# Output projection of a two-layer decoder trunk: the last weight block of two token tiles held back, and some weight remainders made on VectorE

## The chip, the cores and the metric

The kernel runs on one core of a Trainium2 chip. The metric is the device time of one execution in microseconds (us).

The engines are named as the profile names them: PE (TensorE, matrix products), PEld (its weight loads), DVE (VectorE), ACT (ScalarE), POOL (GpSimd) and SP (SyncE, which here issues all DMA transfers). Each engine works through its own instructions strictly in order and waits at the first one whose inputs or buffers are not ready.

## The reference

Two layers run over 1024 tokens of 1024 channels. Each layer mixes tokens with four groups of heads (two gated linear recurrences, latent attention, a delta rule), and then channels with a gated MLP. The change touches only the place between the two, here cut to that:

```python
def reference(x, ...):
    for l in range(DEPTH):                       # 2 layers
        h = rms_norm(x, pre_mix_g[l])
        z = h @ w_in[l]
        ...
        mix = jnp.concatenate([o_a, o_b, o_c, o_d], axis=-1) @ w_out[l]   # (1024, 1024) @ (1024, 1024)
        x = x + rms_norm(mix, post_mix_g[l])
        h = rms_norm(x, pre_ffn_g[l])
        y = conv_glu_ffn(h, ffn_w_gate[l], ffn_w_up[l], ffn_conv_w[l], ffn_w_down[l])
        x = x + rms_norm(y, post_ffn_g[l])
    return x
```

Everything is float32. The change concerns `@ w_out[l]`, the two normalisations behind it, and through them the start of the MLP.

## The kernel before, in words

**Precision.** A float32 operand is split into two parts of a type that PE multiplies fast: a high part, made by a cast on ACT (`split`, L197), and a remainder, operand minus high part, made by a subtraction on POOL unless another engine is passed (L198). `mm3` (L209) then makes one product as three matmuls: high times high, high times remainder, remainder times high. A weight block costs one DMA (tile `wst`, two buffers), one cast and one subtraction (both into tiles `wr`), all called from `weight`.

**Tiling of the output projection** (in `mixing`). Tokens are taken in two halves `hf` of four tiles `t` of 128 tokens; the 1024 output columns in two halves `ch` of 512; the 1024 rows of the weight in four blocks `q` of 256 rows, each two steps `k` of 128. One (`hf`, `ch`) is 4 x 4 x 2 x 3 = 96 matmuls into four PSUM banks, one for each token tile; a layer has four of these, 384 matmuls. In three of the four the loop runs over `q` outside and `t` inside, so that each weight block serves all four token tiles. In the last one (`hf` = `ch` = 1) it runs over `t` outside, so that the token tiles end one after the other and their normalisation can start. A weight block is asked for at its first use. Its `wr` tiles take turns in four buffers for each of two pools, so that the cast of a block waits until PE has finished with the block four places earlier.

**Before each half** PE transposes the mixed heads (`split_T`): per token tile two groups of four transposes into a `pm` bank (four such banks), whose high part ACT casts (L317) and whose remainder DVE subtracts (L318), into tiles `f`.

**Behind each token tile**, once its last block is done: ACT copies the PSUM bank (L1188) and sums squares (L230); POOL (first column half) or DVE (second) multiplies by a gain (`half`, L1162); a reciprocal root is made by a small DVE instruction (L238) and a small POOL one (L239); DVE adds the residual (`post_res`, L328), SP stores it. Then comes the norm in front of the MLP (`prenorm_steps`): squares on ACT (L224), reciprocal root (L246 on DVE, L247 on POOL), product on DVE (L286, tile `jh`), eight transposes on PE (L219), copies on DVE or ACT (L301, L305, L307), and for tiles of the first half a cast (ACT) and a subtraction (POOL, `h` L198). The MLP's first products follow on PE; later ones need sums of these tiles (`combine_s2`, tiles `s2h`, `s2l`).

**What sets the order.** The code gives the order of calls only. A scheduler puts every engine's instructions in a fixed order from its own estimates before the program runs, so that a change of the loop or of an engine also moves other instructions.

Of the kernel before, what the change touches and what calls it, by code (L numbers as in the profile page):

```python
# [128 lines left out]
class Body:  # L129
# [67 lines left out]
        self.marks["hi"] = self.nc.scalar.copy(out=hi, in_=src)  # L197
        (eng or self.nc.gpsimd).tensor_tensor(out=lo, in0=src, in1=hi.bitcast(F32), op=ALU.subtract)  # L198

    def weight(self, src, shape, pool="w"):  # L200

        st = self.load(src, shape)
        hi, lo = (self.t(pool, "wr", 4, shape, F32R) for _ in range(2))
        self.split(hi, lo, st)
        return hi, lo

    def mm3(self, out, a, b, start, stop, onto=False):
# [860 lines left out]
    def mixing(self, l, hT, x_src, x_dst):  # L1068
        nc = self.nc
# [89 lines left out]
        def half(y, n, ss):  # L1159
            self.squares(y, n, ss, self.t("f", "fc", 1, None, BF16))  # L1160
            sl = slice(n * 512, (n + 1) * 512)
            (nc.vector if n else nc.gpsimd).tensor_tensor(out=y[:, sl], in0=y[:, sl], in1=gpost[:, sl], op=ALU.mult)  # L1162

        for hf in range(2):
            mT = []
            for t in range(4):
                m = [self.t("m", "f", NFS, [128, 8, 128], F32R) for _ in range(2)]
                self.split_T(lambda k: groups[k // 2][hf][:, t, k % 2 * 128:k % 2 * 128 + 128],
                             lambda q: tuple(p[:, 4 * q:4 * q + 4, :] for p in m))
                mT.append(m)  # L1170
            y = [self.t("z", "z", 8) for _ in range(4)]
            ss = {}
            for ch in range(2):
                cs = slice(ch * 512, (ch + 1) * 512)
                ps = [self.ps([128, 512], "pd") for _ in range(4)]
                ws = [None] * 4

                for t, q in ((t, q) for t in range(4) for q in range(4)) if hf and ch else (
                        (t, q) for q in range(4) for t in range(4)):
                    if (hf, ch, q, t) == (0, 0, 2, 0):  # L1180
                        gpost, gpre = self.gain(l, 1), self.gain(l, 2)
                    if ws[q] is None:
                        ws[q] = self.weight(self.I["wo"][l, ch, q], [128, 2, 512], "m" if q % 2 else "w")
                    for k in range(2):
                        self.mm3(ps[t], tuple(p[:, q * 2 + k, :] for p in mT[t]), tuple(w[:, k, :] for w in ws[q]),
                                 q == 0 and k == 0, q == 3 and k == 1)
                    if q == 3:
                        ev = nc.scalar.copy(out=y[t][:, cs], in_=ps[t])  # L1188
                        if ch == 0:
                            ss[t] = self.t("c", "s2", 8, [128, 2])  # L1190
                            half(y[t], 0, ss[t])
                        else:
                            waiting.append((hf * 4 + t, y[t], ev, ss[t]))

                    if waiting and (t == 3 if hf == 0 or ch == 0 else q == 3) and (hf or q == 3):

                        tt, yt, ev, sq = waiting.pop(0)
                        half(yt, 1, sq)
                        behind[:] = [self.last_sq] if tt > 4 else []
                        self.step(late)  # L1200
                        x = self.post_res(tt, yt, yt, self.rstd2(sq), x_src, x_dst, ev)
                        late.append(self.prenorm_steps(tt, x, gpre, hT2, "f", behind))
                        next(late[-1])
# [496 lines left out]
```

## Time and profile before

| | |
|---|---|
| device time, median of 3 runs | 2949.01 us (2946.44 to 2950.11) |
| the profiled execution, its own device time | 2954.27 us |
| its span, first to last instruction | 2952.5 us |
| PE busy | 2741.6 us, 93% of the span |
| DVE, ACT, POOL busy | 1822.8, 1327.9, 1231.8 us |
| output projection of layer 0, first matmul to first MLP matmul | 713.97 to 822.58 us |
| the same of layer 1 ends at | 2286.92 us |

The span is that of one profiled execution; around it lie 1.8 us. All rows below are of that execution, with times in us from the start of the span.

### The profile page before, as it was taken

To read this page: it belongs to the slowest core of one execution; us is meant where nothing else is said; L and a number is where in the kernel's file an instruction comes from. 1 tells how busy PE (TensorE), PEld (TensorE's weight loads), DVE (VectorE), ACT (ScalarE), POOL (GpSimd) and SP (SyncE) were. 2 spreads that over 40 slices of the span, in tenths; PEclk is the share of its full clock that TensorE was granted. 3 is DMA by queue.
4 is the path that set the end of the run, shared out by engine and by line. 5 is a ranking of instruction groups with operands and counts; after the bars stand their busy time and mean duration, and the time that the engine had idled before them with its cause. 6 is when DMAs were issued, how large, how long until landed. Compare 5 with 4: busy or idle time off the path is not lost. (4 is left out here: it accounts for less than half of the span.)

```text
span 2952.5 us, 39980 instructions
## 1 busy us (share of the span) xinstructions
PE 2741.6 (93%) x14928; PEld 2227.2 (75%) x14928; DVE 1822.8 (62%) x2638; ACT 1327.9 (45%) x2422; POOL 1231.8 (42%) x1030
## 2 busy tenths in 40 slices
PE   7889888899999999999988997988999899999998
PEld 5688676677777888888767875866777688888887
DVE  4764433895487777764556643349935777776645
ACT  4423334655464444454444233355555544444443
POOL 4522453454666454310155225534446755443001
PEclk9999989999999999999999998999999999999999
DMA  5331553112433233376534316421234332223765
GB/s 187 137 108 66 181 190 112 54 60 102 139 122 121 99 102 108 118 264 198 173 137 149 101 56 218 164 101 54 72 103 140 125 118 100 100 99 104 261 194 192
DMA packets 162673, 386.01 MB, mean 131 GB/s; under 512 B 25488, under 2 KB 37040, under 8 KB 162480
## 3 DMA queue, kind: packets, MB, share of 16 engines
q1 hardware_dynamic: 162480, 383.47, 38.9%
q8 instruction: 117, 1.92, 0.3%
q14 instruction: 76, 0.62, 0.1%
HBM read 273.76 MB, written 109.64 MB: 130 GB/s over the span
## 5 line engine op out<-in xcount | busy, mean ns | idle before, releaser
L209 PE MATMUL pd<-h,wr 128*128 128x512 f32 x2608 | 665.0, 405 | 36.4 <-ACT wr L197 27.7
L198 POOL TENSOR_TENSOR wr<-wst,wr 128x512 fp32r<-128x512 f32 (+1 forms) x188 | 353.9, 1886 | 644.8 <-ACT wr L197 635.2
L209 PEld LDWEIGHTS pd<-h,wr 128*128 128x128 f32 x2608 | 492.6, 191 | 155.9 <-ACT wr L197 29.3
L197 ACT CAST wr<-wst 128x512 fp32r<-128x512 f32 (+1 forms) x260 | 196.7, 760 | 314.1 <-PE pd L209 203.9
L209 PE MATMUL pd<-wr,h 128*128 128x256 f32 x1920 | 250.8, 293 | 0.8 <-issue 0.8
L209 PEld LDWEIGHTS pd<-wr,h 128*128 128x128 f32 x1920 | 243.5, 200 | 2.5 <-issue 1.1
L209 PE MATMUL pm<-h,wr 128*128 128x512 f32 x864 | 230.1, 393 | 1.5 <-DVE x L1396 1.5
L198 DVE TENSOR_TENSOR h<-st,h 128x1024 fp32r<-128x1024 f32 x120 | 152.4, 1273 | 120.9 <-ACT h L197 119.8
L209 PE MATMUL pd<-wr,f 128*128 128x512 f32 x768 | 185.4, 398 | 11.6 <-POOL wr L198 10.6
L209 PEld LDWEIGHTS pm<-h,wr 128*128 128x128 f32 x864 | 162.0, 188 | 39.2 <-DVE x L1396 2.5
L197 ACT CAST h<-st 128x1024 fp32r<-128x1024 f32 x120 | 125.7, 1049 | 146.2 <-PE pd L209 83.0
L209 PE MATMUL pd<-h 128*128 128x512 f32 x816 | 185.6, 389 | 0.0
L209 PEld LDWEIGHTS pd<-wr,f 128*128 128x128 f32 x768 | 143.7, 189 | 45.0 <-POOL wr L198 12.4
L209 PEld LDWEIGHTS pd<-h 128*128 128x128 f32 x816 | 153.2, 188 | 31.8
L1334 DVE SCALAR_TENSOR_TENSOR g<-z,pp,g 128x512 f32<-128x512 f32 x176 | 164.3, 933 | 20.8 <-ACT g L1332 18.0
L209 PE MATMUL pm<-h 128*128 128x512 f32 x720 | 166.2, 391 | 0.5 <-DVE h L198 0.5
L1455 POOL TENSOR_TENSOR y<-y,gb 128x512 f32<-128x512 f32 x24 | 38.2, 1598 | 304.2 <-ACT fc L230 179.3
L209 PEld LDWEIGHTS pm<-h 128*128 128x128 f32 x720 | 135.6, 189 | 29.1 <-DVE h L198 1.0
L215 PE MATMUL pm<-g,g 128*128 128x128 f32 (+1 forms) x672 | 121.4, 329 | 30.9 <-issue 12.9
L215 PEld LDWEIGHTS pm<-g,g 128*128 128x128 f32 x672 | 99.4, 201 | 59.1 <-issue 28.9
L1552 POOL TENSOR_TENSOR d<-d,d 128x512 f32<-128x512 f32 x64 | 109.4, 1709 | 54.4 <-DMA d<-in_wgu_dram 49.0
L209 PE MATMUL pd<-hs,wr 128*128 128x512 f32 x528 | 128.4, 393 | 1.4 <-ACT x L1400 1.4
(364 smaller groups left out, 5428.0 us busy)
## 6 DMA issues: line engine op xcount, KB each, us to landing
st<-gd SPq DMA_DIRECT2D x144, 256.0 KB, 3.2
gd<-g SPq DMA_DIRECT2D x88, 256.0 KB, 2.0
d<-in_wdn_dram SPq DMA_DIRECT2D x40, 512.0 KB, 5.4
td<-d SPq DMA_DIRECT2D x40, 512.0 KB, 2.6
st<-td SPq DMA_DIRECT2D x80, 256.0 KB, 3.6
ust<-in_wgu_dram SPq DMA_DIRECT2D x36, 512.0 KB, 3.8
wst<-in_wgu_dram SPq DMA_DIRECT2D x36, 512.0 KB, 3.6
st<-in_wdn_dram SPq DMA_DIRECT2D x68, 256.0 KB, 3.5
```

Of the source, the lines that this page charges most:

```text
L197: self.marks["hi"] = self.nc.scalar.copy(out=hi, in_=src)
L198: (eng or self.nc.gpsimd).tensor_tensor(out=lo, in0=src, in1=hi.bitcast(F32), op=ALU.subtract)
L209: mm = lambda x, y, **k: self.nc.tensor.matmul(out, lhsT=x, rhs=y, skip_group_check=onto, **k)
L215: self.nc.tensor.matmul(out, lhsT=lhsT, rhs=rhs, start=start, stop=stop)
L1334: nc.vector.scalar_tensor_tensor(out=c, in0=x[:, j:j + 512], scalar=w(j), in1=c, op0=ALU.mult, op1=ALU.add)
L1455: (dve if last and n else pool).tensor_tensor(out=y[t][:, c], in0=y[t][:, c], in1=g_post[:, c], op=ALU.mult)
L1552: sub = lambda o, x, y: nc.gpsimd.tensor_tensor(out=o, in0=x, in1=y, op=ALU.subtract)
```

## The change

The loop of the last quarter (`hf` = `ch` = 1) takes blocks 0 to 2 for token tile 0, then for token tile 1, then block 3 for both; token tiles 2 and 3 go as before. `weight` gets an argument for the engine that makes the remainder: POOL for blocks 0 to 2 in the second half of the tokens, DVE for the eight blocks of the first half and for block 3 of both column halves in the second. So 10 of a layer's 16 weight remainders move from POOL to DVE.

```diff
-    def weight(self, src, shape, pool="w"):
+    def weight(self, src, shape, pool="w", eng=None):
 
         st = self.load(src, shape)
         hi, lo = (self.t(pool, "wr", 4, shape, F32R) for _ in range(2))
-        self.split(hi, lo, st)
+        self.split(hi, lo, st, eng)
         return hi, lo
...
-                for t, q in ((t, q) for t in range(4) for q in range(4)) if hf and ch else (
+
+                for t, q in [(t, q) for t in (0, 1) for q in range(3)] + [(0, 3), (1, 3)] + [
+                        (t, q) for t in (2, 3) for q in range(4)] if hf and ch else (
                         (t, q) for q in range(4) for t in range(4)):
...
-                        ws[q] = self.weight(self.I["wo"][l, ch, q], [128, 2, 512], "m" if q % 2 else "w")
+                        ws[q] = self.weight(self.I["wo"][l, ch, q], [128, 2, 512], "m" if q % 2 else "w",
+                                            nc.gpsimd if hf and q < 3 else nc.vector)
```

PE, the end of the first column of work in the last quarter, layer 0, before (`pd_6859` and `pd_6860` are the banks of token tiles 0 and 1; `wr_6889`/`wr_6890` are high part and remainder of block 2, `wr_6901`/`wr_6902` of block 3, `wr_6865` is block 0; `f_6560`/`f_6561` are tile 0's own parts; `jh_6791` is a token tile of the first half):

```order
L209 MATMUL pd_6859<-wr_6889,f_6561 128x512
L209 MATMUL pd_6859<-wr_6901,f_6560 128x512
L209 MATMUL pd_6859<-wr_6902,f_6560 128x512
L209 MATMUL pd_6859<-wr_6901,f_6561 128x512
L209 MATMUL pd_6859<-wr_6901,f_6560 128x512
L209 MATMUL pd_6859<-wr_6902,f_6560 128x512
L209 MATMUL pd_6859<-wr_6901,f_6561 128x512
L219 MATMUL pm_6915<-cf,jh_6791 128x128 x4
L219 MATMUL pm_6923<-cf,jh_6791 128x128 x4
L209 MATMUL pd_6860<-wr_6865,f_6576 128x512
```

The same place of the changed kernel, where block 3 is `wr_6919`/`wr_6920` and 18 matmuls of token tile 1 stand ahead of it (the last of them is the first row):

```order
L209 MATMUL pd_6860<-wr_6889,f_6577 128x512
L209 MATMUL pd_6859<-wr_6919,f_6560 128x512
L209 MATMUL pd_6859<-wr_6920,f_6560 128x512
L209 MATMUL pd_6859<-wr_6919,f_6561 128x512
L209 MATMUL pd_6859<-wr_6919,f_6560 128x512
L209 MATMUL pd_6859<-wr_6920,f_6560 128x512
L209 MATMUL pd_6859<-wr_6919,f_6561 128x512
L219 MATMUL pm_6933<-cf,jh_6791 128x128 x4
L219 MATMUL pm_6941<-cf,jh_6791 128x128 x4
L209 MATMUL pd_6860<-wr_6919,f_6576 128x512
```

The block 3 products of token tile 0 now stand 36 instead of 18 matmuls behind the start of the quarter, and those of tile 1 six matmuls and eight transposes behind them.

POOL at the same place, before (`z_6624` to `z_6627` are the four token tiles of the second half, first 512 columns):

```order
L198 TENSOR_TENSOR h_6201<-h_6197,h_6200 128x4x128
L1162 TENSOR_TENSOR z_6624<-z_6624,gb_6334 128x512
L1162 TENSOR_TENSOR z_6625<-z_6625,gb_6334 128x512
L1162 TENSOR_TENSOR z_6626<-z_6626,gb_6334 128x512
L198 TENSOR_TENSOR wr_6902<-wst_6899,wr_6901 128x1024
L1162 TENSOR_TENSOR z_6627<-z_6627,gb_6334 128x512
L198 TENSOR_TENSOR h_6199<-h_6194,h_6198 128x4x128
```

And of the changed kernel:

```order
L198 TENSOR_TENSOR h_6201<-h_6197,h_6200 128x4x128
L1162 TENSOR_TENSOR z_6624<-z_6624,gb_6334 128x512
L1162 TENSOR_TENSOR z_6625<-z_6625,gb_6334 128x512
L1162 TENSOR_TENSOR z_6626<-z_6626,gb_6334 128x512
L1162 TENSOR_TENSOR z_6627<-z_6627,gb_6334 128x512
L198 TENSOR_TENSOR h_6199<-h_6194,h_6198 128x4x128
```

The remainder of block 3 (`wr_6902`) has left POOL's queue; on DVE its successor `wr_6920` stands behind three one-column instructions (L232) of the same quarter.

DVE at the border between the two halves, where the eight transposed groups of the second half are taken out of their `pm` banks (L318, `f_6561` to `f_6609`), the difference (- before, + changed):

```order
-L318 TENSOR_TENSOR f_6561<-pm_6562,f_6560 128x512
 L318 TENSOR_TENSOR f_6561<-pm_6569,f_6560 128x512
-L328 SCALAR_TENSOR_TENSOR z_6267<-z_6267,rs_6672,x_6675 128x1024
 L318 TENSOR_TENSOR f_6577<-pm_6578,f_6576 128x512
 L318 TENSOR_TENSOR f_6577<-pm_6585,f_6576 128x512
 L318 TENSOR_TENSOR f_6593<-pm_6594,f_6592 128x512
 L318 TENSOR_TENSOR f_6593<-pm_6601,f_6592 128x512
+L328 SCALAR_TENSOR_TENSOR z_6267<-z_6267,rs_6672,x_6675 128x1024
```

The first group (`pm_6562`) is now transposed near the start of the first half and taken out before the border, and the residual addition L328 stands behind five of the other groups instead of ahead of them.

## Rows read from the trace of the kernel before

**Rows 1.** The page: span, busy times, one group of instructions (mean ns).

```profile
span 2952.5 us, 39980 instructions
PE 2741.6 (93%) x14928; PEld 2227.2 (75%) x14928; DVE 1822.8 (62%) x2638; ACT 1327.9 (45%) x2422; POOL 1231.8 (42%) x1030
...
L198 DVE TENSOR_TENSOR h<-st,h 128x1024 fp32r<-128x1024 f32 x120 | 152.4, 1273 | 120.9 <-ACT h L197 119.8
```

**Rows 2.** Windows, layer 0's last quarter: PE, PEld, DVE, ACT, POOL busy; PEclk; DMA.

```profile
796.00:799.60 3.60, 0.00 (x0) 0.00 (x0) 0.00 (x0) 0.00 (x0) 3.60 (x4) 1.00 0.00 0
799.60:803.60 4.00, 3.98 (x15) 3.40 (x16) 0.96 (x2) 1.70 (x4) 1.20 (x1) 0.59 0.40 131
803.60:822.50 18.90, 18.90 (x95) 15.68 (x94) 14.11 (x17) 9.75 (x20) 12.52 (x11) 1.00 0.33 112
```

**Rows 3.** Timeline of PE, output projection: start, us, instruction [idle before <-what ended it].

```profile
716.38 43.79 PE L209 MATMUL pd<-wr,f 128*128 128x512 f32 x189 [1.48 <-POOL wr L198]
...
762.41 0.74 PE L209 MATMUL pd<-wr,f 128*128 128x512 f32 x2 [0.50 <-ACT f L317]
764.69 0.66 PE L219 MATMUL pm<-cf,z 128*128 128x128 f32 x4 [1.54 <-DVE f L318]
...
768.48 0.66 PE L219 MATMUL pm<-cf,z 128*128 128x128 f32 x4 [1.06 <-DVE f L318]
...
799.62 1.97 PE L209 MATMUL pd<-wr,f 128*128 128x512 f32 x5 [3.84 <-POOL wr L198]
801.39 1.91 PE L219 MATMUL pm<-cf,jh 128*128 128x128 f32 x8
802.95 6.14 PE L209 MATMUL pd<-wr,f 128*128 128x512 f32 x24
808.93 1.03 PE L219 MATMUL pm<-cf,jh 128*128 128x128 f32 x8
809.72 5.78 PE L209 MATMUL pd<-wr,f 128*128 128x512 f32 x24
...
2263.99 2.00 PE L209 MATMUL pd<-wr,f 128*128 128x512 f32 x5 [3.82 <-POOL wr L198]
```

**Rows 4.** Timelines of ACT and POOL around block 3 of the last quarter.

```profile
792.35 1.05 ACT L197 CAST wr<-wst 128x1024 fp32r<-128x1024 f32 x1
...
793.51 3.75 POOL L1162 TENSOR_TENSOR z<-z,gb 128x512 f32<-128x512 f32 x3
797.22 2.34 POOL L198 TENSOR_TENSOR wr<-wst,wr 128x1024 fp32r<-128x1024 f32 x1
```

**Rows 5.** Timeline of DVE: the residual addition twice, at the border of the halves.

```profile
759.42 1.28 DVE L328 SCALAR_TENSOR_TENSOR z<-z,rs,x 128x1024 f32<-128x1024 f32 x1 [0.67 <-POOL rs L239]
...
765.14 2.68 DVE L328 SCALAR_TENSOR_TENSOR z<-z,rs,x 128x1024 f32<-128x1024 f32 x1
```

**Rows 6.** Timelines of ACT, POOL and DVE behind token tile 0, last quarter.

```profile
801.63 0.59 ACT L1188 COPY z<-pd 128x512 f32<-128x512 f32 x1 [7.61 <-PE pd L209]
...
803.90 3.00 POOL L198 TENSOR_TENSOR h<-h,h 128x512 fp32r<-128x512 f32 x2 [3.10 <-ACT h L197]
...
809.13 0.59 ACT L1188 COPY z<-pd 128x512 f32<-128x512 f32 x1 [4.45 <-PE pd L209]
...
812.42 1.28 DVE L286 SCALAR_TENSOR_TENSOR jh<-z,rs,gb 128x1024 f32<-128x1024 f32 x1 [0.60 <-POOL rs L247]
```

**Rows 7.** Timelines of POOL and PE, start of the MLP, layer 0 and layer 1.

```profile
850.30 0.58 POOL L1331 COPY tails<-z 128x2 f32<-128x2 f32 x1 [4.19 <-DVE z L1396]
851.90 0.80 PE L209 MATMUL pd<-s2h,wr 128*128 128x512 f32 x1 [4.24 <-ACT s2h L197]
879.09 2.96 PE L209 MATMUL pm<-h,wr 128*128 128x512 f32 x12
...
2314.66 10.81 POOL L1331 COPY tails<-z 128x2 f32<-128x2 f32 x1 [4.19 <-DVE z L1396]
2350.08 2.94 PE L209 MATMUL pm<-h,wr 128*128 128x512 f32 x12
```

## The prediction

> **What bounds the kernel now.** I read the page first: PE is busy for 2741.6 of 2952.5 us [rows 1], so only a stretch in which PE stands still, or runs at its lower clock, can give time back, and the other engines matter where PE waits for them. The change touches nothing but the output projection of each layer, so next I read PE's timeline there. In layer 0 the reader is to see five waits [rows 3]: 1.48 us at the start for the first weight remainder from POOL; 0.50, 1.54 and 1.06 us at the border between the token halves, for casts and subtractions that free transpose banks; and 3.84 us in the last quarter, again for a remainder from POOL. Layer 1 has the last one too, with 3.82 us [rows 3]. In 796.0 to 799.6 us PE, DVE and ACT all do nothing and POOL alone is busy [rows 2].
>
> Then POOL and ACT ahead of that wait [rows 4]. The high part of block 3 is cast from 792.35 to 793.40 us; then POOL spends 793.51 to 797.26 us on three gain products that nobody waits for yet, and only then makes the remainder, which ends at 799.56 us. PE goes on at 799.62 us. So the wait is a matter of POOL's order, not of the DMA or the cast.
>
> The clock row follows: 1.00 in the wait, 0.59 on average in the 4 us behind it, 1.00 after that [rows 2]. PE fell to its 1.2 GHz level behind the wait and came back to 2.4 GHz about three us later.
>
> Last I read what lies behind the projection: PE waits 4.24 us for `s2h` at 851.90 us [rows 7], the end of a chain through ACT, DVE and POOL that starts at the last token tile. A gain in the projection is worth only as much as this chain moves with it.
>
> **The change part by part, for one layer.**
>
> *The wait in the last quarter.* In the changed order block 3 is needed after 36 matmuls instead of 18. A matmul in an unbroken run takes 43.79 / 189 = 0.232 us [rows 3], so it would be needed 4.2 us after PE now stops (799.62 - 3.84 = 795.78), at 799.9 us. Ready it is earlier: the cast still ends at 793.4, and the subtraction takes 1.27 us on DVE, by 120 instructions of that size [rows 1], against 2.34 us on POOL [rows 4]; DVE is idle there [rows 2]. That is 794.7 us, five us to spare. The wait of 3.84 us goes; a bound on the other side is that DVE is held up by more than five us, for which no row speaks. What stands behind the new DVE instruction is one one-column instruction and then the copies of the next transposes, which come seven us later: costs nothing.
>
> *The clock behind it.* The next 5 matmuls took 1.97 us against 5 x 0.232 and some 0.25 for the last one's drain, 1.41: 0.56. The 8 transposes took 1.91 against 1.03, the 24 matmuls 6.14 against 5.78, by the next ones of their kind [rows 3]. Sum 0.56 + 0.88 + 0.36 = 1.8 us, which goes with the wait (bounds 0 and 1.8).
>
> *The start.* The first remainder moves from POOL (2.34 us [rows 4]) to DVE (1.27 us [rows 1]): 1.1 us of the 1.48 us wait. One matmul and four transposes, moved up ahead of it, fill what is left. I take 1.1 (bounds 0, if DVE's two late subtractions behind it now hold PE, and 1.48).
>
> *The border of the halves.* PE waits 0.50 + 1.54 + 1.06 = 3.1 us [rows 3]. The first wait goes, since the first transposed group is now taken out beforehand, so that six matmuls of token tile 0 can run at once. The second stays: PE reaches it sooner, but its bank is freed behind the same norm chain on DVE; I put 1.9 us. The third goes: the bank it waited for was freed behind the residual addition that took 2.68 us [rows 5] and is now freed ahead of it. Four transposes fewer stand there, at 1.03 us for 8 about 0.4 us. So 3.1 - 1.9 + 0.4 = 1.6 us (bounds 0 and 3.1).
>
> *The seven other remainders of the first half* meet an almost idle DVE and no PE wait: the 189 matmuls run without a break [rows 3]; POOL gains 7 x 2.34 us that no one waits for. Nothing. On SP one residual load moves ahead of one weight load and one behind, in a stretch without a wait for a DMA: nothing.
>
> *What is late next.* So far PE gains 3.84 + 1.8 + 1.1 + 1.6 = 8.3 us. But token tile 0 now ends 18 matmuls later, and PE asks for its normalised rows (transposes of `jh`) 8 transposes, 6 matmuls, 8 transposes and 24 matmuls behind: 0.8 + 1.4 + 0.8 + 5.6 = 8.6 us after its end. Today the chain from the copy at 801.63 us to the end of the product L286 at 812.42 + 1.28 takes 12.1 us, hidden because a whole tile more lies between [rows 6]. It will be shorter: ACT held the chain back until 809.13 us, where the next tile's copy stood in front of the squares [rows 6], and that tile now ends 2.2 us after tile 0. Two subtractions on POOL of 3.00 us together still stand in front of the reciprocal root [rows 6], and now two tiles share DVE. Adding up the steps I get 10.6 to 11.2 us, so a new wait of 2.0 to 2.6 us; I take 2.3. Bounds: 0, and 12.1 - 8.6 = 3.5 us. Whether the clock falls behind it is open: 1.54 us did not bring it down, 3.84 us did [rows 2, 3]; that would be up to 1.8 us more. I leave it out of the sum and in the range.
>
> *Handing on.* 8.3 - 2.3 = 6.0 us for a layer. The rest of the chain to `s2h` hangs on the token tiles' ends and on loads that are issued behind them, nothing on a fixed time, so I let 6.0 us pass on whole.
>
> **Sum.** Two layers, 12.0 us: the profiled execution would go from 2954.3 to 2942.3 us. The median of the runs shown is 5.3 us under that execution, so the forecast is 2949.0 - 12.0 = **2937.0 us**.
>
> **A lock that could undo part of it.** At the start of the MLP POOL copies two columns (`tails`). In layer 0 that took 0.58 us, in layer 1, at the same distance from the wait in the projection (50.68 and 50.67 us), 10.81 us [rows 3, 7], while DVE ran without a gap. What it cost: from the wait in the projection to the twelve matmuls that follow later is 879.09 - 799.62 = 79.47 us in layer 0 and 2350.08 - 2263.99 = 86.09 us in layer 1, 6.6 us more. Likewise the residual addition took 1.28 us alone and 2.68 us where POOL was at work [rows 5]. The Trainium skill (SBUF — State Buffer, Who interferes with whom) says that a DVE instruction with two SBUF inputs and a GpSimd instruction that reads SBUF shut each other out for the whole instruction, whoever starts first. The trace agrees in kind. By that rule every remainder moved to DVE becomes one that can shut POOL out, which speaks against the change; by the rows of the first half, where POOL has little left to do, it costs nothing.
>
> **The rivals.**
> (A) The forecast, 12 us less, its own range 2933 to 2941 us: 50%.
> (B) The norm chain of tile 0 is short enough and no new wait comes: 2 x 8.3 = 16.6 us, 2932.4 us. For it speaks that three of the chain's steps were waiting in line today; against it, that two tiles now come at once. 12%.
> (C) As A, but a `tails` copy falls the other way than in a typical run. One more is shut out: 2937.0 + 6.6 = 2943.6 us, 14%. One fewer: 2930.4 us, 8%. The order there is unchanged, only the moment shifts, and layers 0 and 1 show that the moment decides.
> (D) The gain ends at the wait for `s2h`: DVE's chain there does not come sooner, and PE waits 4.24 + 6.0 us instead. No change, 2949 us. For it: PE waits there today. Against it: DVE had 18.90 - 14.11 us of idle time in the last quarter [rows 2], so it follows the tiles. 10%.
> (E) Slower: with two tiles at once DVE works without a gap while POOL's small reciprocal root (L239) needs its turn, and is shut out as the copy was, for 10.81 - 0.58 = 10.2 us [rows 7]. It decides from 6.0 us in each layer on; at 10.2 us the sum is 2 x (10.2 - 6.0) = 8.4 us, 2957.4 us. Against it: DVE has had gaps in this stretch every few us. 6%.
>
> **How the numbers follow.** Predicted is A. A difference of 0.2%, 5.9 us, is about what a measurement of this kernel can tell from no change. Faster by more (below 2943.1 us) are A, B, the good side of C and almost half of its bad side: 0.74. Within 0.2% are D and the rest of C: 0.20. Slower is E: 0.06. For the range I leave out D above 2946 and E, and the tail under 2927 us: 2927 to 2946 us holds A, B and both sides of C.
>
> **What the profile will show.** Right: no PE wait of over 1 us for a POOL `wr` in the projection, and a granted clock of 1.00 there in the last quarter; the three waits at the border down to one of about 1.9 us; a wait of about 2.3 us for `jh` L286 ahead of the transposes behind token tile 2; the first MLP matmul of layer 0 some 6 us earlier than 822.58 us, the one on `s2h` some 6 us earlier than 851.90 us. Wrong: a wait for block 3 that merely names DVE instead of POOL; a `jh` wait of over 3.5 us, or a clock of 0.5 behind it; `s2h` at 851.9 us as before; a `tails` copy of 10 us in both layers.

## The result and the profile after

The changed kernel takes 2934.59 us (median of 4 runs, 2932.39 to 2936.43) where the kernel before took 2949.56 us beside it (4 runs, 2946.44 to 2955.0). The ratio is 0.9943, with a 95% interval of 0.9927 to 0.9958: faster by 15 us. The forecast was 2937.0 us.

The page after, against [rows 1]; the profiled execution took 2936.43 us:

```profile
span 2934.6 us, 39974 instructions
PE 2736.2 (93%) x14928; PEld 2224.1 (76%) x14928; DVE 1838.8 (63%) x2658; ACT 1328.4 (45%) x2422; POOL 1187.8 (40%) x1010
```

With the 20 remainders that moved, POOL has lost 44 us of work and DVE has gained 16 us. PE lost only 5.4 us of busy time; the rest of the 18 us by which the span is shorter was waiting.

PE's timeline of the output projection after, layer 0 and then layer 1, against [rows 3, 7] (start, us, instruction, and in brackets the idle time before it and what ended it):

```profile
713.52 1.43 PE L209 MATMUL pd<-wr,f 128*128 128x512 f32 x4
...
715.15 43.53 PE L209 MATMUL pd<-wr,f 128*128 128x512 f32 x188
...
763.16 0.66 PE L219 MATMUL pm<-cf,z 128*128 128x128 f32 x4 [1.32 <-DVE f L318]
...
774.20 1.03 PE L219 MATMUL pm<-cf,jh 128*128 128x128 f32 x8
...
781.44 15.44 PE L209 MATMUL pd<-wr,f 128*128 128x512 f32 x66
796.71 1.03 PE L219 MATMUL pm<-cf,jh 128*128 128x128 f32 x8
...
799.76 5.81 PE L209 MATMUL pd<-wr,f 128*128 128x512 f32 x24
808.03 1.06 PE L219 MATMUL pm<-cf,jh 128*128 128x128 f32 x8 [2.46 <-DVE jh L286]
...
815.27 5.72 PE L209 MATMUL pd<-h,wr 128*128 128x512 f32 x24
...
844.76 0.79 PE L209 MATMUL pd<-s2h,wr 128*128 128x512 f32 x1 [4.23 <-ACT s2h L197]
...
858.18 1.22 PE L209 MATMUL pd<-s2h,wr 128*128 128x512 f32 x2 [6.84 <-POOL wr L198]
...
2170.94 1.43 PE L209 MATMUL pd<-wr,f 128*128 128x512 f32 x4
...
2265.41 1.06 PE L219 MATMUL pm<-cf,jh 128*128 128x128 f32 x8 [2.46 <-DVE jh L286]
...
2272.63 5.73 PE L209 MATMUL pd<-h,wr 128*128 128x512 f32 x24
```

The wait at the start is gone, the border has one wait instead of three, and 66 matmuls run without a break through the place where block 3 was waited for. In return there is one new wait, of 2.46 us for `jh`, ahead of the transposes behind token tile 2. The clock did not fall behind it (columns as in [rows 2], PEclk third from the end):

```profile
781.40:796.70 15.30, 15.30 (x69) 12.46 (x68) 5.60 (x10) 8.25 (x18) 14.02 (x9) 1.00 0.46 156
796.70:808.00 11.30, 8.87 (x47) 7.15 (x45) 7.89 (x12) 7.05 (x15) 6.57 (x7) 1.00 0.24 74
808.00:815.30 7.30, 7.27 (x41) 6.22 (x41) 6.68 (x7) 4.51 (x9) 4.70 (x5) 1.00 0.50 175
```

From here on a **stretch** is the time from the first matmul of a layer's projection to the first MLP matmul (the first `pd<-h,wr` row), both starts read from PE's timeline. Before it is 822.58 - 713.97 = 108.6 us, and 108.6 us in layer 1; after it is 815.27 - 713.52 = 101.7 us, and 2272.63 - 2170.94 = 101.7 us. It holds all four quarters and the new wait. In the traces of kernels with the same order of the projection it repeats to 0.1 us (table below), where the whole time spreads over 4 to 18 us in the runs of one kernel; so it is the better measure of this change.

The chain of token tile 0's normalisation, ahead of the new wait; timelines of ACT, DVE and POOL after, in order of time, against [rows 4, 6]:

```profile
788.21 1.05 ACT L197 CAST wr<-wst 128x1024 fp32r<-128x1024 f32 x1
789.29 1.23 DVE L198 TENSOR_TENSOR wr<-wst,wr 128x1024 fp32r<-128x1024 f32 x1 [0.86 <-ACT wr L197]
...
796.91 0.59 ACT L1191 COPY z<-pd 128x512 f32<-128x512 f32 x1 [7.03 <-PE pd L209]
798.84 2.81 POOL L198 TENSOR_TENSOR h<-h,h 128x512 fp32r<-128x512 f32 x2 [3.42 <-ACT h L197]
801.60 0.55 POOL L239 TENSOR_TENSOR rs<-rs,nhalf 128x1 f32<-128x1 f32 x1
802.19 2.31 DVE L328 SCALAR_TENSOR_TENSOR z<-z,rs,x 128x1024 f32<-128x1024 f32 x1 [1.89 <-POOL rs L239]
804.53 1.06 ACT L224 ACTIVATE jh<-z 128x1024 f32<-128x1024 f32 x1 [3.49 <-DVE z L328]
806.02 0.55 POOL L247 TENSOR_TENSOR rs<-rs,nhalf 128x1 f32<-128x1 f32 x1 [2.59 <-DVE rs L238]
806.60 1.28 DVE L286 SCALAR_TENSOR_TENSOR jh<-z,rs,gb 128x1024 f32<-128x1024 f32 x1 [0.61 <-POOL rs L247]
```

From the copy to the end of L286 it takes 806.60 + 1.28 - 796.91 = 11.0 us. The two subtractions on POOL that nobody hurries for (798.84) stand in front of the reciprocal root L239 again.

### The profile page after: what moved, and what is told of

Its sections match the earlier page's. It is cut to its first block, busy times and chain, and to the rows that moved or that the text cites. A ratio compares the mean times of both kernels' runs of the same rounds, so it can differ in the third digit from the quotient of the medians.

```text
span 2934.6 us, 39974 instructions
## 1 busy us (share of the span) xinstructions
PE 2736.2 (93%) x14928; PEld 2224.1 (76%) x14928; DVE 1838.8 (63%) x2658; ACT 1328.4 (45%) x2422; POOL 1187.8 (40%) x1010
## 5 line engine op out<-in xcount | busy, mean ns | idle before, releaser
L198 POOL TENSOR_TENSOR wr<-wst,wr 128x512 fp32r<-128x512 f32 (+1 forms) x168 | 307.9, 1837 | 616.1 <-ACT wr L197 606.7
L1337 DVE SCALAR_TENSOR_TENSOR g<-z,pp,g 128x512 f32<-128x512 f32 x176 | 164.2, 933 | 20.4 <-ACT g L1335 17.9
L198 DVE TENSOR_TENSOR wr<-wst,wr 128x512 fp32r<-128x512 f32 (+1 forms) x92 | 95.9, 1043 | 101.5 <-ACT wr L197 101.5
```

Of the source, the lines that this page charges most:

```text
L1337: nc.vector.scalar_tensor_tensor(out=c, in0=x[:, j:j + 512], scalar=w(j), in1=c, op0=ALU.mult, op1=ALU.add)
```

## The experiments

"Before" is the median of the kernel before, run in the same set; the stretches are those of the profiled execution.

| kernel | median us | before | ratio (95%) | stretch, layer 0 / 1 |
|---|---|---|---|---|
| changed | 2934.59 | 2949.56 | 0.9943 (0.9927 to 0.9958) | 101.7 / 101.7 |
| e1 engine moves only | 2930.78 | 2954.23 | 0.9929 (0.9910 to 0.9949) | 99.1 / 99.1 |
| e2 order only | 2947.89 | 2954.23 | 0.9983 (0.9970 to 0.9997) | 105.6 / 105.5 |
| e3 block 3 on DVE only | 2945.45 | 2954.23 | 0.9971 (0.9956 to 0.9986) | 105.8 / 103.0 |
| e4 first half on DVE only | 2944.66 | 2954.23 | 0.9969 (0.9957 to 0.9981) | 104.8 / 105.0 |
| e5 changed, again | 2939.70 | 2953.82 | 0.9952 (0.9937 to 0.9967) | 101.7 / 101.7 |
| e6 as e1, again | 2933.84 | 2953.82 | 0.9932 (0.9918 to 0.9946) | 99.1 / 99.1 |
| e7 changed, `tails` on ACT | 2936.57 | 2953.82 | 0.9937 (0.9923 to 0.9951) | 101.7 / 101.7 |
| e8 as e1, `tails` on ACT | 2929.76 | 2953.82 | 0.9923 (0.9909 to 0.9936) | 99.1 / 99.1 |
| e9 as e1, other additions | 2935.87 | 2952.78 | 0.9947 (0.9930 to 0.9965) | 99.1 / 99.1 |
| e10 as e8, other additions | 2931.11 | 2952.78 | 0.9931 (0.9915 to 0.9947) | 99.1 / 99.1 |
| e11 as e1, third time | 2933.26 | 2952.78 | 0.9939 (0.9921 to 0.9956) | 99.1 / 99.1 |

### Which part clears the wait: the order or the engine?

The prediction priced the later place of block 3 and its move to DVE as one term. Its own numbers held a rival: the remainder on DVE would end at 794.7 us, and PE came to it at 795.8 us even in the old order. Four kernels take the two apart.

**e1**, the changed kernel with the old loop:

```diff
-                for t, q in [(t, q) for t in (0, 1) for q in range(3)] + [(0, 3), (1, 3)] + [
-                        (t, q) for t in (2, 3) for q in range(4)] if hf and ch else (
+                for t, q in ((t, q) for t in range(4) for q in range(4)) if hf and ch else (
```

> Edit: the ten remainders stay on DVE, but the loop of the last quarter is the old one, token tile by token tile, so nothing is held back. Theory 1 (holding back is what clears the wait for block 3): block 3 is needed after 18 matmuls again and the wait comes back, over 1 us for `wr` from DVE instead of POOL, with the clock behind it; 2940 to 2945 us, slower than the changed kernel by 5 to 10 us. Theory 2 (the engine alone clears it, since the subtraction on DVE ends about 794.7 us and PE comes to it at 795.8 us in the trace before): no wait over 0.3 us for block 3, no clock drop, and the wait for `jh` of 2.46 us behind token tile 2 goes too; 2 x 2.5 = 5 us under the changed kernel, about 2930 us. PE now reaches block 3 some 3.3 us earlier against the trace before, by the shorter start and border, which is the weak place of Theory 2: if DVE's end does not move with it, a wait of up to 2 us is left there.

Timelines of PE and DVE in e1, layer 0:

```profile
712.61 1.43 PE L209 MATMUL pd<-wr,f 128*128 128x512 f32 x4
...
780.51 11.28 PE L209 MATMUL pd<-wr,f 128*128 128x512 f32 x48
788.34 1.23 DVE L198 TENSOR_TENSOR wr<-wst,wr 128x1024 fp32r<-128x1024 f32 x1 [0.87 <-ACT wr L197]
...
804.46 1.04 PE L219 MATMUL pm<-cf,jh 128*128 128x128 f32 x8
...
811.70 5.73 PE L209 MATMUL pd<-h,wr 128*128 128x512 f32 x24
```

Theory 2 holds. Token tile 0 runs through all its 24 matmuls inside an unbroken run of 48, although the remainder of block 3 ends only at 789.57 us. Of these 48 matmuls 24 belong to the quarter before, 18 to blocks 0 to 2, and the first of block 3 takes only the high part; so the remainder is asked for at 780.51 + 43 x 11.28 / 48 = 790.6 us, 1.0 us behind its end. And the transposes at 804.46 us wait for no `jh`. The stretch is 99.1 us in both layers, 2.6 us shorter than with the block held back. The time, 2930.78 us, is what Theory 2 asked for, though the kernel before took 4.7 us more in this set than in the first.

**e2**, the opposite: the new loop, all remainders on POOL.

```diff
-                                            nc.gpsimd if hf and q < 3 else nc.vector)
+                                            nc.gpsimd)
```

> Edit: the new loop order, but all 16 remainders of a layer on POOL as before. Theory 1 (holding back clears the wait): the remainder ends at 799.6 us as before and is needed at 799.9 us, so the wait is under 0.5 us and the clock holds, worth 5.6 us in a layer; the start (1.48 us) and the border (3.1 us) wait as before, and `jh` waits some 2.5 us more: 3.1 us a layer, about 6 us under the kernel before, 2943 us. Theory 2 (the engine is what counts): a wait for block 3 of over 1 us stays in place, and no gain is left after the `jh` wait, 2948 to 2952 us.

PE's timeline in e2, layer 0:

```profile
713.61 43.86 PE L209 MATMUL pd<-wr,f 128*128 128x512 f32 x189 [1.47 <-POOL wr L198]
...
782.93 15.50 PE L209 MATMUL pd<-wr,f 128*128 128x512 f32 x66
...
809.59 1.06 PE L219 MATMUL pm<-cf,jh 128*128 128x128 f32 x8 [2.46 <-DVE jh L286]
```

As Theory 1 had it: the order clears the wait for block 3 too (66 matmuls without a break), though only just: POOL makes the remainder from 794.56 us in 2.40 us, and it is asked for at 782.93 + 61 x 15.50 / 66 = 797.3 us. The start waits as before, and `jh` costs 2.46 us. The stretch is 3.0 us shorter than before, the time 6.3 us. So the order alone clears the wait, and so do the ten moves alone; the order is paid for with `jh`, the moves with nothing that the stretch shows.

**e3** moves nothing but block 3 of the second half, in the old loop; PE's order is that of before.

```diff
-                                            nc.gpsimd if hf and q < 3 else nc.vector)
+                                            nc.vector if hf and q == 3 else nc.gpsimd)
```

> Edit: the old loop order, and only block 3 of the two quarters of the second half of the tokens has its remainder made on DVE; PE's order is that of the kernel before, instruction by instruction. Theory 2 (the engine alone clears the wait): 3.84 us and the 1.8 us at the low clock behind it go in both layers, nothing else changes, no `jh` wait: 2 x 5.6 = 11.3 us under the kernel before, about 2938 us. Theory 1 (it has to be held back as well): the wait stays, over 1 us, 2944 us or more.

PE's timeline in e3, layer 0 (with DVE's remainder of block 3), then layer 1:

```profile
766.40 2.91 PE L209 MATMUL pd<-wr,f 128*128 128x512 f32 x6
...
792.79 4.41 PE L209 MATMUL pd<-wr,f 128*128 128x512 f32 x18 [0.73 <-ACT z L1190]
797.42 0.50 PE L209 MATMUL pd<-wr,f 128*128 128x512 f32 x1 [0.22 <-ACT wr L197]
797.41 1.23 DVE L198 TENSOR_TENSOR wr<-wst,wr 128x1024 fp32r<-128x1024 f32 x1 [0.89 <-ACT wr L197]
798.69 1.43 PE L209 MATMUL pd<-wr,f 128*128 128x512 f32 x5 [0.76 <-DVE s L232]
...
2256.62 1.42 PE L209 MATMUL pd<-wr,f 128*128 128x512 f32 x5 [0.76 <-DVE s L232]
```

The result lies between the theories, in time too (8.8 us under the kernel before, where Theory 2 asked for 11.3): 3.84 us became 0.76 us in both layers, and the clock stayed up behind it (1.42 us for the 5 matmuls instead of 1.97). The releaser named is a one-column instruction on DVE (L232); what PE needs there is the remainder just ahead of it in DVE's queue, which ends at 797.41 + 1.23 = 798.64 us. In layer 1 the stretch is 5.6 us shorter than before, but not by block 3 alone: the third wait at the border, 1.07 us in layer 1 before, is gone from that trace too. Layer 0 is some 2.8 us longer than layer 1: six matmuls at the border took 2.91 us, at a granted clock of 0.75 to 0.83 in 764 to 772 us, and ACT, which had waited until 782.38 us for the load of a weight block, came late with the bank (0.73 us) and the cast (0.22 us). So the move of block 3 alone is late by 0.76 us. With the other eight moves (e1) PE's and ACT's order changes as well, and nothing is left; which of these changes closes the gap no run shows.

**e4** moves only the eight remainders of the first half, in the old loop.

```diff
-                                            nc.gpsimd if hf and q < 3 else nc.vector)
+                                            nc.gpsimd if hf else nc.vector)
```

> Edit: the old loop order, and only the eight remainders of the first half of the tokens on DVE; block 3 stays on POOL. The start and the border are all that change. By the account of the trace after, they gave some 3.5 us a layer on PE, but the wait for block 3 stands behind them: if POOL's end of that remainder (799.56 us) follows PE, 2 x 3.5 = 7 us under the kernel before, about 2942 us; if POOL's order there is set by work that does not start earlier, the wait of 3.84 us grows by what the border gave, and nothing is left, 2948 to 2950 us.

Timelines of POOL and PE in e4, layer 0:

```profile
785.16 3.74 POOL L1162 TENSOR_TENSOR z<-z,gb 128x512 f32<-128x512 f32 x3
788.86 2.34 POOL L198 TENSOR_TENSOR wr<-wst,wr 128x1024 fp32r<-128x1024 f32 x1
791.26 1.53 PE L209 MATMUL pd<-wr,f 128*128 128x512 f32 x5 [3.89 <-POOL wr L198]
```

The first alternative: the wait stays at 3.89 us, as long as before, because POOL's queue starts earlier with PE. Start and border alone give 3.8 and 3.6 us of the stretch, and 9.6 us of the time where 7 were expected. e4 and e1 differ in the code only in the engine of block 3, so this move is worth 104.8 - 99.1 = 5.7 us, and 5.9 us in layer 1, wait and clock together.

### Is the hold-back a loss in the whole time, and what is a `tails` copy worth?

The next four ran in one set. `tails` is the copy on POOL that the prediction's rival C was about.

```diff
-                    nc.gpsimd.tensor_copy(out=ends[f], in_=x[:, 512:514])
+                    nc.scalar.copy(out=ends[f], in_=x[:, 512:514])
```

> Edit: none, the changed kernel as it is, timed beside the three others of this set. Expected: 0.9943 of the kernel before again, with the interval of 0.9927 to 0.9958 seen first. Which of the two layers has its `tails` copy shut out by DVE may differ; the two layers' projections, 131.2 us from the first matmul to the first one on `s2h`, may not, by more than 0.3 us.

> Edit: as the first experiment (ten remainders on DVE, old loop order), to be timed beside the changed kernel. Theory 2 (holding back is not needed, and only brings the wait for `jh`): in the traces the stretch to `s2h` is 128.4 and 128.8 us against 131.2 us, so 2 x 2.6 = 5.2 us under the changed kernel, 0.9925 of the kernel before. Theory 1 (in time the two are alike, since what comes earlier is waited for at `tails` or later): within 2 us of the changed kernel, 0.994.

> Edit: the changed kernel with the copy of two columns (`tails`) on ACT instead of POOL. Theory A (a DVE without a gap shuts POOL's copy out, and PE then waits 7 us for the `wr` behind it): no such wait in either layer; 10 us shorter from the first matmul on `s2h` to the first on `hs` in a layer that was shut out, of which the trace of after against before says 3.5 us last to the end; with half the copies shut out in a usual run, 3.5 to 7 us under the changed kernel, 2928 to 2931 us. Theory B (whatever POOL starts next is shut out in its place): a `wr` subtraction on POOL takes 10 us there instead, PE waits as before, and the time stays within 2 us of the changed kernel.

> Edit: the old loop order with the ten remainders on DVE, and `tails` on ACT. If the two gains add up (2 x 2.6 us by the order, 3.5 to 7 us by the copy): 9 to 12 us under the changed kernel, about 2923 us, 0.990 of the kernel before, and the best of all. If the copy is worth nothing, as the first of these two alone, 2929 us.

The stretches repeat to 0.1 us. Up to the first matmul on `s2h`, e5 took 131.2 us in layer 0 as expected, but 131.8 us in layer 1, over the 0.3 us allowed: one more wait for `jh`, of 0.53 us, stands in the MLP's first products there. Side by side the kernel without the hold-back is 5.9 us faster (2933.84 against 2939.70 us), 6.8 us with `tails` on ACT (2929.76 against 2936.57 us), where the stretches say 2 x 2.6 = 5.2 us. The intervals of each pair still overlap, and the means of the six runs differ by 5.8 and 4.6 us with standard errors of 2.3 and 1.7 us; what carries the conclusion is that both pairs and both layers' stretches agree.

With `tails` moved the medians are 3.1 us (e7 against e5) and 4.1 us (e8 against e6) lower, about the low end of what Theory A asked for. By the means it is 4.3 and 3.1 us, with standard errors of 2.2 and 1.8 us, so neither pair by itself is clear of the noise. The timelines of e7 say why it is not more (POOL and PE, layer 0):

```profile
848.50 12.61 POOL L198 TENSOR_TENSOR wr<-wst,wr 128x512 fp32r<-128x512 f32 x3 [6.85 <-ACT wr L197]
857.79 1.22 PE L209 MATMUL pd<-s2h,wr 128*128 128x512 f32 x2 [3.79 <-POOL wr L198]
```

The copy is off POOL, and now the `wr` subtractions are the ones that are shut out: the first of the three took 9.24 us by itself, all three 12.6 us, and PE waits 3.79 us, where it waited 6.84 us after. Theory B was right that the next instruction on POOL is shut out in the copy's place, but not that PE waits as long as before; Theory A was right about part of the gain, if the 3 to 4 us hold. e8 has the lowest ratio of the study, 9.9 us under the changed kernel as expected (9 to 12 us), though its ratio is 0.9923 and not 0.990, and its interval overlaps those of e1, e6 and e11.

### What lets POOL through?

In the traces of before, after, e1 and e11 the copy that was shut out ended within 0.15 us of the moment when DVE came to its first SCALAR_TENSOR_TENSOR (L1337 of the changed kernel) behind a row of TENSOR_TENSORs; timelines of POOL and DVE after, layer 0:

```profile
843.16 10.82 POOL L1334 COPY tails<-z 128x2 f32<-128x2 f32 x1 [4.18 <-DVE z L1399]
...
846.63 1.88 DVE L1272 TENSOR_TENSOR h<-h,h 128x512 f32<-128x512 f32 x3
...
853.86 0.73 DVE L1337 SCALAR_TENSOR_TENSOR g<-z,pp,g 128x512 f32<-128x512 f32 x1
```

So e9 and e10 make four of these TENSOR_TENSORs instructions of the other kind, e9 in e1's kernel and e10 in e8's:

```diff
-                dve.tensor_tensor(out=s1[:, k, :], in0=s1[:, k, :], in1=a22[:, k, :], op=ALU.add)
+                dve.scalar_tensor_tensor(out=s1[:, k, :], in0=s1[:, k, :], scalar=1.0, in1=a22[:, k, :], op0=ALU.mult, op1=ALU.add)
```

> Edit: old loop order with the ten remainders on DVE, and the four additions of DVE in the MLP's start (`s1` plus `a22`) written as multiply by 1.0 and add, which is another kind of DVE instruction with the same result; every engine's order stays as it was. Theory A (a row of DVE instructions of the one kind, TENSOR_TENSOR, shuts POOL out as long as it lasts; POOL gets through at the first instruction of another kind): `tails` on POOL takes about 3.6 us instead of 10.8 us, up to the first of these additions, PE's wait for the POOL `wr` behind it falls from 7.0 us to under 3 us, and some 4 to 7 us a layer come back there, of which 2 to 4 us last: 4 to 8 us under the same kernel without this edit. Theory B (it is the two SBUF inputs that shut POOL out, of either kind of instruction): `tails` takes 10.8 us as before, and the time stays within 2 us.

> Edit: as the one ahead of it, and `tails` on ACT. Theory A: the three `wr` subtractions on POOL that follow take 5 to 8 us instead of 12.6 us, PE's wait for them falls from 4.6 us to under 2 us; 2 to 4 us a layer, 4 to 8 us under the kernel with `tails` on ACT alone, the best of all at about 2922 to 2926 us. Theory B: 12.6 us as before, no change against 0.9923.

> Edit: the first experiment once more, as the base of the two others of this set: 0.993 of the kernel before, `tails` shut out in one or both layers.

Timelines of POOL in e9, layer 0, and then of DVE and POOL in e10, layer 0:

```profile
836.45 5.39 POOL L1333 COPY tails<-z 128x2 f32<-128x2 f32 x1 [4.19 <-DVE z L1398]
...
843.94 1.88 DVE L1271 SCALAR_TENSOR_TENSOR h<-h,h 128x512 f32<-128x512 f32 x3
843.14 12.60 POOL L198 TENSOR_TENSOR wr<-wst,wr 128x512 fp32r<-128x512 f32 x3 [6.85 <-ACT wr L197]
851.16 1.75 DVE L1336 SCALAR_TENSOR_TENSOR g<-z,pp,g 128x512 f32<-128x512 f32 x1
852.84 6.83 DVE L198 TENSOR_TENSOR s<-h,h 128x512 fp32r<-128x512 f32 x4
855.70 6.83 POOL L198 TENSOR_TENSOR wr<-ust,wr 128x512 fp32r<-128x512 f32 x4
```

Theory A falls: in e10 POOL's first subtraction (843.14 us, 9.23 us by itself) sat through all four of the rewritten additions, the three at 843.94 us and one later, up to L1336 at 851.16 us. The three subtractions took 12.60 us, as in e8 (12.62), and PE waited 4.26 us for them where the theory asked for under 2. In e9 the copy took 5.39 us in layer 0, let through right behind the additions, but 10.81 us again in layer 1, past the same four. The kind alone does not decide. Why POOL comes through at that instruction each time (L1337, in e10 L1336; its scalar is a column of a tile and not a constant, and it follows work of ACT) stays open. Nor did any run take the row of DVE instructions away: that DVE is what holds POOL is read from the times alone. In time e9 and e10 gained nothing: 2935.87 against 2933.26 us for e11, and a ratio of 0.9931 against 0.9923 for e8.

## Why the prediction was right, and where its terms were off

**The wait in the last quarter and the clock behind it.** Forecast 3.84 + 1.8 = 5.6 us; measured alone (e1 against e4) 5.7 and 5.9 us. Right in size. The forecast "five us to spare" was right too: the remainder ended at 789.29 + 1.23 = 790.5 us and was needed at about 795.7 us, behind 61 of the 66 matmuls. What was not asked is whether all five were needed. They were not: 1.0 us to spare, without the hold-back (e1), did as well.

**Start and border.** Forecast 1.1 + 1.6 = 2.7 us; measured alone (e4) 3.8 and 3.6 us. This is the term that was mis-sized. The start gave what was forecast: from the first matmul to the end of the first half's 192nd it took 716.38 + 43.79 - 713.97 = 46.2 us before and 715.15 + 43.53 - 713.52 = 45.2 us after, the four transposes included. The border gave more: from there to the first transposes of `jh` it took 18.2 us before (they began at 778.40 us) and 15.5 us after, 2.7 us instead of 1.6. Of that, 0.6 us is the wait that stayed, 1.32 us where 1.9 was put down; the remaining half microsecond I can't put to one row.

**The new wait for `jh`.** Forecast 2.3 us within 0 and 3.5; measured 2.46 us in both layers, in the forecast place, with the clock at 1.00 behind it. It costs 2.6 us of the stretch (changed against e1). That the clock would stay up was left open, and one reason given for it is weaker than it looked: the prediction read that 1.54 us of waiting did not bring the clock down. In the traces of before, e2 and e3 the same wait at the border, 1.53 or 1.54 us, stands six times; five times the granted clock stayed at 1.00, and in e3, layer 0, it fell to 0.72 in the two us from 765.11 us and 0.62 in the next three. Rival B, no new wait, is out; so is E: L239 took 0.55 us.

**Handing on.** The first matmul on `s2h` came at 844.76 instead of 851.90 us, with the same wait of 4.23 us ahead of it: the chain moved with the tiles, as forecast, and D is out. Sum per layer: 3.7 + 5.8 - 2.6 = 6.9 us, against the forecast 6.0. These three are differences of the same stretches, so they must add up to the measured 108.6 - 101.7; what tests them is the time. Twice 6.9 is 13.8 us, and the two comparisons in time gave 15.0 and 14.1 us.

**Rival C.** In this one profiled execution the copies changed places: layer 0's was shut out (10.82 us) and layer 1's was not, so they nearly cancel. In the ten traces of kernels with `tails` on POOL, before included, this copy stands 20 times: 13 took 10.8 us, one 5.39 us, and six under 1 us. In before and in both traces of the changed kernel it is one of two each time, so a matter of the moment, as the prediction said, and not of the change. In e1, e2 and e6 it is two of two; whether a kernel shifts the odds, so few cases can't tell. Its price was put too high. PE's rows before (layer 0, layer 1) and after (layer 0):

```profile
912.68 5.82 PE L209 MATMUL pm<-h,wr 128*128 128x512 f32 x24 [1.01 <-DVE x L1396]
...
2380.54 5.71 PE L209 MATMUL pm<-h,wr 128*128 128x512 f32 x24
...
909.01 5.71 PE L209 MATMUL pm<-h,wr 128*128 128x512 f32 x24
```

At `s2h` PE stood 851.90 - 844.76 = 7.1 us ahead of before; behind the shut-out copy, at these 24 matmuls, 3.7 us. So 3.5 us of net loss and not 6.6, mostly because four later waits for ACT and DVE, of 0.44 to 1.35 us, that the trace before shows between 858 and 913 us, are not there after the long one. The trace before held this price already: from the wait in the projection to these 24 matmuls it took 912.68 - 799.62 = 113.1 us in layer 0 and 2380.54 - 2263.99 = 116.6 us in layer 1, 3.5 us more. The prediction compared the layers at 879.09 us, ahead of three of the four waits.

One slip in the chances: almost half of C's bad side (0.14) is some 0.06 and not the 0.04 that stands in the sum, so "faster" comes to 0.76 and "within 0.2%" to 0.18.

## What to carry to other kernels

When a change both moves a producer to a faster queue and moves its consumer back, price the two apart: here the order alone or the ten moves alone cleared the wait, and doing both cost 2.6 us a layer for nothing. Holding a tile's last block back delays everything that hangs on the end of that tile, so count from its new end to the next consumer of its results before you do it. And compare a stretch between two fixed instructions rather than whole times: it repeated to 0.1 us here, where whole runs of one kernel spread over 4 to 18 us.

## What was not expected of the hardware

A POOL copy of two columns was shut out, by its times behind DVE, not for one instruction but for a row of 18 without a gap: 10.81 or 10.82 us in each of 13 cases. In the six short cases the same copy, begun at the same point of the same row, took 0.58 us and ended with the one DVE instruction that was running (before, layer 0: 850.30 + 0.58 = 850.88 us, DVE's L1252 ended at 850.83 us). The Trainium skill (SBUF — State Buffer, Who interferes with whom) says that whoever starts first keeps the other out for its whole instruction. The six short cases agree with that. The 13 long ones go further: there POOL's turn did not come at the end of an instruction. What decides between the two is open. Once POOL was through, the two took turns: in e10 four subtractions on DVE (from 852.84 us) and four on POOL (from 855.70 us) took 6.83 us each, 1.7 us apiece. After, the same four on DVE (from 854.52 us) took 2.48 us, and three subtractions on POOL beside them (from 853.94 us) 7.56 us: there POOL was the one that waited.
